# Layer 0's feed-forward network of a two-layer backbone in eighths of Strassen's products, mixed with the second matrix

## The chip, the cores and the metric

The kernel runs on one core of a Trainium2 chip. The metric is the device time of one execution in microseconds (us). A core has five engines that work through queues of their own, in order: TensorE (PE, with the weight loads PEld), VectorE (DVE), ScalarE (ACT), GpSimd (POOL) and SyncE (SP), which here issues the transfers. Line numbers such as L313 are those of the kernel file.

## The reference

Two layers over 512 latent tokens and 256 context tokens of width 1024. Each has a token mixer (windowed attention in layer 0, differential attention in layer 1) and a feed-forward network with a squared relu, hidden width 4096. All is float32.

```python
def sqrelu_mlp(h, w1, w2):
    return jnp.square(jax.nn.relu(h @ w1)) @ w2
...
        mod_x = jax.nn.silu(c) @ w_ada[i] + b_ada[i]
        sh1, sc1, g1, sh2, sc2, g2 = jnp.split(mod_x[:, None, :], N_MOD, axis=-1)
...
        x = layer_norm(alpha * x + g1 * ax, ln1_g[i], ln1_b[i])
        fx = sqrelu_mlp(x * (1.0 + sc2) + sh2, mlp_w1[i], mlp_w2[i])
        x = layer_norm(alpha * x + g2 * fx, ln2_g[i], ln2_b[i])
```

The context tokens go through layer 0 in the same way, with modulation of their own; layer 1 gives the latent tokens only. So layer 0's network works on 768 tokens, layer 1's on 512.

## The kernel before

**Products.** TensorE takes each float32 operand as a high and a low part: `wsplit` loads 128x1024 of a weight (`w_raw`), ScalarE rounds it to the high part `w_h` (L264), and VectorE subtracts to get the low part `w_l` (L313). `mm3` (L323) then makes three matmuls: high by high, high by low, low by high (L324 to L326).

**Layer 0's network, `mlp` (L681).** The 4096 hidden values are 32 blocks of 128, in four chunks of eight. For each chunk the first matrix is applied block by block (`h_ps<-hx0m`, 8 steps of the inner dimension, tokens in two cuts of 384), the result goes through relu on ScalarE, a square on VectorE (first chunk) or GpSimd (the others) and a split into `hid`. Then `tok_product` applies the second matrix for that chunk: for each half of the output columns (512) and each of the six token blocks, into `y_ps`, with four weights. The sums over chunks are kept in `fx` (VectorE adds `fx<-y_ps,fx`), the residual in `acc`.

**Layer 1's network, `mlp_pipe` (L768)**, works otherwise. Hidden blocks 0 to 5 are plain products. From there on, pairs `q` = 3 to 15 of hidden blocks take Strassen's seven block products in place of eight: the pair's 256 hidden values, the 1024 inner values and the tokens are each halved, sums of the weight's blocks are made on GpSimd (`w_sum`, `w_raw`), sums of the tokens' blocks once at the start (`token_sums`), and each half weight `w_half` of 512 columns is split on ScalarE and VectorE. The second matrix is mixed in: `pair` runs its products with "half-steps" of the second matrix between them (a half-step is one weight by one token block, six matmuls of 512 columns).

**The modulation's rows, `ada_rows` (L405).** While layer 0's network runs, VectorE computes the modulation of layer 0's last gate and of all of layer 1: 56 units of a 128x1024 piece of `w_adaT`, each multiplied by a row of silu(c) (`cB`) and reduced, once for the latent tokens or twice (context as well, then the first result goes to `ada_pr`). It is a generator; each `next` on it issues one unit: one transfer of 512 KB and one or two reductions. `mlp` calls it once for six of eight blocks in a chunk, and in the first four token blocks of each half of the second matrix.

**What sets the order.** `Flow` is a planner: jobs are generators that yield conditions, and its model of times (a clock `T`, an entry for each engine) decides which job goes on next. The order of TensorE's instructions is as the planner writes them. All engines take their queues in the order in which they were issued. Rings (`Ring`) and tile pools limit how far loads run ahead: three `w_raw` tiles, four pairs of `w_h` and `w_l`, and the modulation's units take their piece from the same three `w_raw` tiles as the weights.

Of the kernel before, what the change touches and what calls it, by code (L numbers as in the profile page):

```python
# [38 lines left out]
NRAW, NH, NQ = 3, 4, 4  # L39
# [195 lines left out]
def hybrid_block(ctx: ExitStack, tc: tile.TileContext, t: dict, out: bass.AP):  # L235
# [51 lines left out]
    rwh, rhalf = Ring(fl, NH), Ring(fl, NQ)  # L287


    xraw = {"n": 0, "pool": None}  # L290

# [113 lines left out]
    def ada_rows(pool, c_rows):  # L405
        cB = [bcast_load(pool, c_rows[s:s + 1], f"cB{s}") for s in range(2)]
        yield
        for l, m in [(0, 5)] + [(1, m) for m in (1, 0, 2, 4, 3, 5)]:
            mod = mods[l][:, m]
            n = 2 if l == 0 or m < 2 else 1  # L410
            for k in range(KT):
                raw, rg, rr = raw_tile()
                d = dma(1024, [rg], out=raw, in_=t["w_adaT"][l, m, k])
                for s in range(n):
                    to = pool.tile([P, D], F32, name="ada_pr", tag="xr", bufs=2) if s == 0 and n == 2 else raw
                    d = dv(1024, [d], nc.vector.tensor_tensor_reduce, out=to, in0=raw, in1=cB[s], scale=1.0, scalar=0.0,
                           op0=ALU.mult, op1=ALU.add, accum_out=mod[:, k, s:s + 1])
                d.ring = rr
                if k == KT - 1:
                    d = ada_bias(l, m, slice(0, KT), mod[:, :, 0:n], mod[:, :, 0:n], d)  # L420
                    if m in (2, 5):
                        fl.add(ada_gate(l, m, d), 0)
                    ada_done.add((l, m))
                yield
# [98 lines left out]
    def ln_job(pool, acc, tb, hx, A, B, ready, st, dep, keep=None):  # L523
# [4 lines left out]
        for q in range(2):  # L528
# [7 lines left out]
            if keep is not None:  # L536
                v = keep.rearrange("p (k t) -> p k t", t=P)[:, 4 * q:4 * q + 4]
            else:
                v = pool.tile([P, 4, P], F32, name="hx_v", tag="tmp", bufs=2)
# [25 lines left out]
    def gated_add(pool, give, acc, half, pt, p, gate, last, scale=1.0):  # L565
        cs_ = slice(half * 512, (half + 1) * 512)
        tm = pool.tile([P, 512], F32, name="g_tmp", tag="tmp", bufs=2)
# [26 lines left out]
    def tok_product(pool, src, W, seq, acc, gates, done=None, st=None, scale=1.0, extra=None, pre={}, sink=None,  # L594
# [5 lines left out]
        for i, (half, tb) in enumerate(seq):  # L600
# [8 lines left out]
            if fine and i == len(seq) - 1:  # L609

                for c in range(2):
# [16 lines left out]
                    tm = pool.tile([P, 256], F32, name="g_tmp", tag="tmp", bufs=2)  # L628
# [52 lines left out]
    def mlp(l, hx, ready, apool, pool, ntok, acc, gates, done, extra, res, XR=0):  # L681
        ntb = ntok // P
        first = [slice(i, i + 256) for i in range(0, ntok, 256)]

        parts = [slice(0, 512)] if ntok <= 512 else [slice(0, ntok // 2), slice(ntok // 2, ntok)]
        fx = [pool.tile([P, D], F32, name="fx", tag="fx", bufs=ntb) for _ in range(ntb)]


        def sum_up(ch, gates):
            def sink(tb, half, pt, p, give):  # L690
                x = fx[tb][:, half * 512:half * 512 + 512]
                if ch == 0:
                    give(ac(512, [p], nc.scalar.copy, out=x, in_=pt))
                    if res:
                        res.pop(0)()
                    return
                d = dv(512, [p], nc.vector.tensor_tensor, out=x, in0=pt, in1=x, op=ALU.add)
                give(d)
                if ch == 2:
                    c = slice(half * 512, half * 512 + 512)  # L700
                    g = gates[0 if tb < NXB else 1][:, c]
                    d = gp(pool2(512), [d], nc.gpsimd.tensor_tensor, out=x, in0=x, in1=g, op=ALU.mult)
                    gp(pool2(512), [d], nc.gpsimd.tensor_tensor, out=acc[tb][:, c], in0=acc[tb][:, c], in1=x, op=ALU.add)
            return sink

        row_gates = gates
        for ch in range(4):
            if l == 0 and ch == 1:
                st2["second"] = True
# [1286 lines left out]
```

## Time and profile before

| | |
|---|---|
| time, median of 3 runs | 1663.5 us (1660.76 to 1663.76) |
| the profiled execution: its time, its span | 1662.87 us, 1661.0 us |
| TensorE, VectorE, ScalarE, GpSimd busy | 1597.7, 1026.7, 726.0, 386.2 us |
| granted clock, mean over the span | 0.992 |
| layer 0's network on TensorE | about 349 to 907 us |
| layer 1's network on TensorE | about 1290 to 1661 us |

Shares of busy time are means over stages with different limits; the views by stretch of time and the waits of one engine tell which engine sets the pace in a stage. The names left of the arrow are what an instruction writes, those right of it what it reads; the engine that ended an idle time stands behind its own arrow.

### The profile page before, as it was taken

The page shows a single profiled execution, that of the slowest core. Times are in us where ns is not written, and L with a number is a line of the kernel's source. Part 1 is how long each engine was busy: PE and PEld are TensorE (multiplying, and loading weights), DVE is VectorE, ACT ScalarE, POOL GpSimd, SP SyncE. Part 2 cuts the span into 40 slices and gives each one's busy share as a digit, 9 for nine tenths or more (in the row PEclk, how much of TensorE's full clock was granted, in tenths as well). Part 3 has the DMA queues.
Part 4 walks back from the last instruction along what each step waited for, and adds up shares of the span by engine and source line. Part 5 has one row for each costly group of instructions (what it writes and reads, how often), then busy time and mean ns, then how long its engine had stood idle before and what let it go on. Part 6 is the DMA issues. An engine that isn't in the chain of part 4 may idle for free.

```text
span 1661.0 us, 24864 instructions
## 1 busy us (share of the span) xinstructions
PE 1597.7 (96%) x9621; PEld 1404.3 (85%) x9621; DVE 1026.7 (62%) x1863; ACT 726.0 (44%) x1528; POOL 386.2 (23%) x342
## 2 busy tenths in 40 slices
PE   7899999999999999999999999999989899999997
PEld 5788777789889889979978999899877789888886
DVE  4655676668855344444346777777665975666576
ACT  3465675362323113212216555556552744445550
POOL 1333454100002101243220122220100022222363
PEclk9999999999999999999999999999999999999999
DMA  9110550524444234334222122211123233333321
GB/s 373 41 51 33 179 178 26 193 81 146 134 151 158 98 127 150 104 114 139 92 77 100 60 72 69 71 48 39 48 74 130 89 127 102 102 102 102 102 77 51
DMA packets 57245, 174.84 MB, mean 105 GB/s; under 512 B 7144, under 2 KB 13096, under 8 KB 57128
## 3 DMA queue, kind: packets, MB, share of 16 engines
q1 hardware_dynamic: 57128, 173.27, 30.9%
q8 instruction: 75, 1.23, 0.3%
q14 instruction: 42, 0.34, 0.1%
HBM read 165.35 MB, written 7.90 MB: 104 GB/s over the span
## 4 chain that ended last, share of the span: by engine, by line
PE 72%; DVE 11%; ACT 5%; issue 5%; DMA 4%; POOL 3%; SPq 0%; DVEq 0%; POOLq 0%; ACTq 0%
PE y_ps L326 9%; PE y_ps L325 9%; PE y_ps L324 9%; PE h_ps L324 7%; PE h_ps L325 7%; PE h_ps L326 7%; PE qkv_ps L324 2%; PE qkv_ps L325 2%; PE qkv_ps L326 2%; PE o_ps L1369 2%; PE s_ps L1685 2%; DVE w_l L313 2%; PE pT_ps L1387 2%; DMA w_raw<-in_w 2%; PE o_ps L1723 1%
## 5 line engine op out<-in xcount | busy, mean ns | idle before, releaser
L264 ACT CAST w_h<-w_raw 128x1024 fp32r<-128x1024 f32 (+1 forms) x159 | 159.0, 1008 | 287.4 <-PE y_ps L326 136.2
L313 DVE TENSOR_TENSOR w_l<-w_raw,w_h 128x1024 fp32r<-128x1024 f32 (+1 forms) x159 | 193.1, 1224 | 146.8 <-ACT w_h L264 146.5
L325 PE MATMUL y_ps<-w_l,hid 128*128 128x512 f32 (+1 forms) x648 | 254.5, 393 | 2.9 <-DVE w_l L313 2.7
L326 PE MATMUL y_ps<-w_h,hid 128*128 128x512 f32 (+1 forms) x648 | 254.4, 393 | 0.3 <-DVE hid L260 0.2
L324 PE MATMUL y_ps<-w_h,hid 128*128 128x512 f32 (+1 forms) x648 | 254.3, 392 | 0.0
L326 PE MATMUL h_ps<-hx0m,w_l 128*128 128x384 f32 (+1 forms) x528 | 176.3, 334 | 1.3 <-DVE w_l L313 1.1
L324 PE MATMUL h_ps<-hx0m,w_h 128*128 128x384 f32 (+1 forms) x528 | 176.3, 334 | 0.0
L325 PE MATMUL h_ps<-hx0m,w_h 128*128 128x384 f32 (+1 forms) x528 | 175.9, 333 | 0.0
L325 PEld LDWEIGHTS y_ps<-w_l,hid 128*128 128x128 f32 x648 | 122.1, 188 | 30.5 <-DVE w_l L313 5.3
L326 PEld LDWEIGHTS y_ps<-w_h,hid 128*128 128x128 f32 x648 | 122.0, 188 | 28.7 <-DVE hid L260 1.2
L324 PEld LDWEIGHTS y_ps<-w_h,hid 128*128 128x128 f32 x648 | 122.2, 189 | 25.5 <-ACT w_h L264 0.2
L268 POOL TENSOR_TENSOR relu<-relu 128x768 f32<-128x768 f32 x24 | 42.7, 1779 | 367.0 <-ACT relu L264 367.0
L324 PE MATMUL qkv_ps<-w_h,hx 128*128 128x384 f32 (+1 forms) x384 | 127.5, 332 | 0.2
L325 PE MATMUL qkv_ps<-w_l,hx 128*128 128x384 f32 (+1 forms) x384 | 122.9, 320 | 0.8 <-DVE w_l L313 0.8
L326 PE MATMUL qkv_ps<-w_h,hx 128*128 128x384 f32 (+1 forms) x384 | 122.5, 319 | 0.0
L268 POOL TENSOR_TENSOR e<-e,sm 128x512 f32<-128x512 f32 (+2 forms) x96 | 92.6, 977 | 109.5 <-DVE sm L260 85.2
L326 PEld LDWEIGHTS h_ps<-hx0m,w_l 128*128 128x128 f32 x528 | 99.7, 189 | 2.5 <-DVE w_l L313 2.5
L324 PEld LDWEIGHTS h_ps<-hx0m,w_h 128*128 128x128 f32 x528 | 99.9, 189 | 0.2
L325 PEld LDWEIGHTS h_ps<-hx0m,w_h 128*128 128x128 f32 x528 | 99.8, 189 | 0.1
L260 DVE TENSOR_TENSOR fx<-y_ps,fx 128x512 f32<-128x512 f32 x68 | 46.7, 687 | 76.8 <-PE y_ps L326 76.8
L260 DVE CUSTOM_DVE_ANT_0 w_raw<-w_raw,cB 128x1024 f32<-128x1024 f32 x56 | 76.0, 1359 | 25.5 <-DMA w_raw<-in_w_adaT 25.3
L268 POOL TENSOR_TENSOR rope<-rope,rope 128x256 f32<-128x256 f32 (+1 forms) x40 | 33.8, 846 | 216.4 <-DVE rope L260 175.2
(252 smaller groups left out, 3713.8 us busy)
## 6 DMA issues: line engine op xcount, KB each, us to landing
w_raw<-in_w SPq DMA_DIRECT2D x128, 512.0 KB, 3.6
w_raw<-in_w_adaT SPq DMA_DIRECT2D x56, 512.0 KB, 3.5
w_raw<-in_w_ada SPq DMA_DIRECT2D x24, 512.0 KB, 4.1
w_raw<-in_b_w SPq DMA_DIRECT2D x32, 384.0 KB, 3.3
raw<-in_w_ada SPq DMA_DIRECT2D x16, 512.0 KB, 9.6
w_raw<-in_a_wq SPq DMA_DIRECT2D x8, 512.0 KB, 4.6
w_raw<-in_a_wo SPq DMA_DIRECT2D x8, 512.0 KB, 4.5
w_raw<-in_b_wo SPq DMA_DIRECT2D x8, 512.0 KB, 3.8
```

The costliest lines, as they stand in the source:

```text
L260: fn(**kw)
L264: fn(**kw)
L268: fn(**kw)
L313: last["split"] = nc.vector.tensor_tensor(**kw)
L324: nc.tensor.matmul(out=o, lhsT=lh, rhs=rh, start=start, stop=False, **kw)
L325: nc.tensor.matmul(out=o, lhsT=lh, rhs=rl, start=False, stop=False, **kw)
L326: last["pe"] = nc.tensor.matmul(out=o, lhsT=ll, rhs=rh, start=False, stop=stop, **kw)
L1369: nc.tensor.matmul(out=po[odd * HD:odd * HD + HD, 0:256], lhsT=vv[:, kb, kvh], rhs=pt_[:, odd * 256:odd * 256 + 256], start=(i == 0), stop ...
L1387: nc.tensor.transpose(out=pp[:, c * P:(c + 1) * P], in_=es[j][:, i * P:(i + 1) * P], identity=ident)
L1685: nc.tensor.matmul(out=sp[:, c * 512:c * 512 + 384], lhsT=qTt[:, tt, hl, qb * P:(qb + 1) * P], rhs=kS[:, tt, c * 384:c * 384 + 384], start ...
L1723: nc.tensor.matmul(out=po[:, qp * 256:(qp + 1) * 256], lhsT=vt[:, kb, vl], rhs=pt_[:, pl, a * 256:a * 256 + 256], start=(kp == 0 and pl == ...
```

## The change

`mlp` is gone, and layer 0 calls `mlp_pipe` too, with 768 tokens. What differs between the layers (buffers, how many half-steps stand in a gap, how early weights are asked for) moves to two small classes, `R0` and `R1`.

- Layer 0's first six hidden blocks are plain products, pairs 3 to 15 take seven products of 12 matmuls of 384 columns. The half-steps per pair are 4, 4 and 4 (2, 2 and 2 for the last pairs).
- The normalised tokens go to `fx` instead of a small buffer; `token_sums` makes the four sums from there. Their high and low parts need room: two take the place of `acc`, one that of a hidden tile, and one overlays a quarter of `hx0m` once the plain products have read it.
- The residual is made early and written to memory outside (`m_spill`, six tiles of 512 KB). At the last pair `tail` opens `acc` anew and reads it back; then the sums so far are multiplied by the gate and added (`fold`, 24 operations on GpSimd).
- `ada_rows` goes in two passes of 512 columns, since `cB` now has half the room. There are still 56 units of 512 KB, but each has two or four reductions of 512 columns, and the second pass adds up. `R.extra()` calls it after every half-step, and once ahead of a pair.
- The weights of the second matrix are asked for singly: one ahead (`R.ahead` is 1 in layer 0), the second just before the next pair.
- The relu's square moves from GpSimd to ScalarE, the four sums of weights per pair are on GpSimd. In layer 1 the last two products of a pair change places, and the last group of half-steps has a third early start.

```diff
     def ada_rows(pool, c_rows):
-        cB = [bcast_load(pool, c_rows[s:s + 1], f"cB{s}") for s in range(2)]
-        yield
-        for l, m in [(0, 5)] + [(1, m) for m in (1, 0, 2, 4, 3, 5)]:
...
+        todo = [(0, 5)] + [(1, m) for m in (1, 0, 2, 4, 3, 5)]
+        for h in range(2):
+            c_ = slice(h * 512, h * 512 + 512)
+            cB = [pool.tile([P, 512], F32, name=f"cB{s}", tag="tmp", bufs=tmpb[0]) for s in range(2)]
...
+                for k in range(0, KT, 2):
+                    raw, rg, rr = raw_tile()
+                    d = dma(1024, [rg], out=raw.rearrange("p (k c) -> p k c", k=2),
+                            in_=t["w_adaT"][l, m, k:k + 2, :, c_].rearrange("k p c -> p k c"))
+                    for s in range(n):
+                        for i in range(2):
+                            src = raw[:, i * 512:i * 512 + 512]
+                            to = src
+                            if s == 0 and n == 2:
+                                to = pool.tile([P, 512], F32, name="ada_pr", tag="tmp", bufs=tmpb[0])
+                            d = dv(512, [d], nc.vector.tensor_tensor_reduce, out=to, in0=src, in1=cB[s], scale=1.0,
+                                   scalar=0.0, op0=ALU.mult, op1=ALU.add, accum_out=mod[:, k + i, s:s + 1])
...
-    def mlp(l, hx, ready, apool, pool, ntok, acc, gates, done, extra, res, XR=0):
...
+        def fold(half, tb, d):
+            cs_ = slice(half * 512, half * 512 + 512)
+            x, g = fx[tb][:, cs_], gates[0 if tb < NXB else 1]
+            d = gp(pool2(512), [d], nc.gpsimd.tensor_tensor, out=x, in0=x, in1=g[:, cs_], op=ALU.mult)
+            gp(pool2(512), [d], nc.gpsimd.tensor_tensor, out=acc[tb][:, cs_], in0=acc[tb][:, cs_], in1=x, op=ALU.add)
...
+        def steps(n):
+            for _ in range(n):
+                for x in ys:
+                    if x == "half":
+                        break
+                    yield x
+                R.extra()
...
+            yield from plain((0, 1), cuts, step=R.step)
+            R.swap()
+            for ft in range(2, 6):
+                yield from plain((ft,), [t1, t2], sums, (3, 3, 2, 1)[ft - 2])
...
         y_weights(0, 0)
-        weights(3, NQ)
-        y_weights(0, 1)
-        yield from steps(ys, 8)()
+        weights(3, 4)
+        y_weights(0, 1, R.ahead)
+        yield from steps(2 * ntb)
         for q in range(3, 16):
...
             def ahead():
-                weights(q + 1, NQ)
-                if q < 15:
-                    y_weights(*((q - 1) // 2, (q - 1) % 2) if q < 14 else (6, 1))
-            yield from pair(q, steps(ys, n), ahead)
-        yield from steps(ys, 99)()
+                weights(q + 1, 4)
+                if q < 14:
+                    y_weights((q - 1) // 2, (q - 1) % 2, R.ahead)
+                elif l or q == 15:
+                    y_weights(6, 1, R.ahead)
+                if q == 15:
+                    R.tail()
+                R.extra()
+            m = R.mixes[q < 14]
+            if q < 15:
+                y_weights((q - 2) // 2, q % 2)
+            yield from pair(q, lambda i: steps(m[i]), ahead)
...
+        class R0:
+            rhalf = Ring(fl, 3)
+            mixes = ((2, 2, 2, 0), (4, 4, 4, 0))
+            p3_first, gate_at, res = True, 16, None
+            ahead, done = 1, 0
...
+            def step(self):
+                tb, self.done = self.done, self.done + 1
+                d = residual(acc[tb], gx, gc, last["pe"])
+                dma(D, [d], out=m_spill[tb], in_=acc[tb])
...
+            def tail(self):
+                p_ = open_top("mlp0c")
+                acc[:] = [p_.tile([P, D], F32, name="acc0", tag="acc", bufs=NTB) for _ in range(NTB)]
+                for tb in range(NTB):
+                    dma(D, [], out=acc[tb], in_=m_spill[tb])
+
+            def extra(self):
+                next(filler, None)
```

How the units stand among VectorE's other work before, in the first chunk of the network (`ISA` rows are reductions, `mods` rows their accumulator reads; the numbers tell tiles apart):

```order
L313 TENSOR_TENSOR w_l_4465<-w_raw_4463,w_h_4464 128x1024
L260 ISA ada_pr_4459,mods0_81<-w_raw_4457,cB0_4318 128x1024
L260 ISA mods0_81 128x1
L260 TENSOR_TENSOR relu_4452<-relu_4452 128x768
L260 ISA w_raw_4457,mods0_81<-w_raw_4457,cB1_4320 128x1024
L260 ISA mods0_81 128x1
L260 TENSOR_TENSOR hid_4057<-relu_4452,hid_4057 128x768
L260 ISA ada_pr_4495,mods0_81<-w_raw_4493,cB0_4318 128x1024
L260 ISA mods0_81 128x1
L260 ISA w_raw_4493,mods0_81<-w_raw_4493,cB1_4320 128x1024
L260 ISA mods0_81 128x1
L313 TENSOR_TENSOR w_l_4535<-w_raw_4533,w_h_4534 128x1024
```

Between two weights stand two units with four reductions. In the changed kernel, on VectorE, the end of what stands ahead of the second weight (`w_l_4826`) of the second group of the second matrix:

```order
L260 ISA ada_pr_4818,mods1_82<-w_raw_4816,cB0_4655 128x512
L260 ISA mods1_82 128x1
L260 ISA ada_pr_4820,mods1_82<-w_raw_4816,cB0_4655 128x512
L260 ISA mods1_82 128x1
L260 ISA w_raw_4816,mods1_82<-w_raw_4816,cB1_4656 128x512
L260 ISA mods1_82 128x1
L260 ISA w_raw_4816,mods1_82<-w_raw_4816,cB1_4656 128x512
L260 ISA mods1_82 128x1
L314 TENSOR_TENSOR w_l_4826<-w_raw_4824,w_h_4825 128x1024
L260 TENSOR_TENSOR w_half_4833<-w_raw_4059,w_half_4833 128x512
```

This is the last of the units; from the square of the last plain block (`relu_4600`) to `w_l_4826` there are 36 reductions. The next such weights are `w_l_5109`, `w_l_5428` and `w_l_5740`, with 28, 40 and 34 reductions ahead of each, counted from the one before; then 14, and none after pair 6.

On SP, the transfers of the same place (`in_w_adaT` are the units, `in_w2` the second matrix, `in_w1` the first) before:

```order
L275 DMA w_raw_4463<-in_w1 128x1024
L275 DMA w_raw_4493<-in_w_adaT 128x1024
L275 DMA w_raw_4527<-in_w_adaT 128x1024
L275 DMA w_raw_4533<-in_w1 128x1024
L275 DMA w_raw_4563<-in_w_adaT 128x1024
```

and in the changed kernel:

```order
L275 DMA w_raw_4786<-in_w_adaT 128x2x512
L275 DMA w_raw_4801<-in_w_adaT 128x2x512
L275 DMA w_raw_4816<-in_w_adaT 128x2x512
L275 DMA w_raw_4824<-in_w2 128x1024
L275 DMA w_raw_4877<-in_w_adaT 128x2x512
L275 DMA w_raw_4892<-in_w_adaT 128x2x512
L275 DMA w_raw_4903<-in_w_adaT 128x2x512
L275 DMA w_raw_4058<-in_w1 128x1024
```

Eleven units stand in a row ahead of `w_raw_4824` there. TensorE reads this weight in the first half-steps after two products of pair 3:

```order
L326 MATMUL y_ps_4870<-w_l_4644,hid_4054 128x512
L327 MATMUL y_ps_4870<-w_h_4643,hid_4054 128x512
L325 MATMUL y_ps_4870<-w_h_4825,hid_4055 128x512
L326 MATMUL y_ps_4870<-w_l_4826,hid_4055 128x512
L327 MATMUL y_ps_4870<-w_h_4825,hid_4055 128x512
```

The first half-step's weight (`w_h_4643`, `w_l_4644`) is followed by the second; the second matmul there needs the low part `w_l_4826`.

More of the change, by code (lines that the diff above doesn't have):

```diff
@@ L991, in last_y, with before @@
             early = []
-            y_weights(6, 1)
-            y_weights(7, 0)
-            for tb in range(2):
+            def before(tb):
                 yield sm_.ok
@@ L1000, in last_y @@
                 early.append((pt, slot))
+            y_weights(6, 1)
+            y_weights(7, 0)
+            yield from before(0)
+            yield from before(1)
+            if not gates:
+                gates.extend((yield from get_gates()))
+                for half in range(2):
+                    for tb in range(ntb):
+                        fold(half, tb, None)
             for tb in range(ntb):
@@ L1006, in last_y @@
                     p = y_half(7, 0, tb, i, pt, i == 0, i == 1, tb == ntb - 1)
[L1007 removed]
+                final(0, tb, pt, p, slot)
             y_weights(7, 1)
+            yield from before(2)
             for tb in range(ntb):
[L1010 to L1011 removed]
+                end = tb == ntb - 1 and l == 1
+                if tb < 3:
                     pt, slot = early[tb]
@@ L1037, in last_y @@
                 done(tb, st[tb], r)
-        def steps(gen, n):
-            def mix():
-                for _ in range(n):
-                    for x in gen:
-                        if x == "half":
-                            break
-                        yield x
-            return mix
-        order = [(c, half, tb) for c in range(7) for half in range(2) for tb in range(ntb)][:-ntb]
-        sums = token_sums()
-        yield from plain(range(4), [slice(i, i + 256) for i in range(0, ntok, 256)])
@@ L1069, in mlp_pipe @@
+        for x in ys:
+            if x != "half":
+                yield x
         yield from last_y()
@@ L1477, in main0 @@
                 scale_inplace(b_, ALPHA)
-            res = [lambda tb=tb: residual(acc[tb], gx, gc, last["pe"]) for tb in range(NTB)]
-            yield from mlp(0, hx, ready, apool, pool, TOK, acc, g2, done2, filler, res, D)
+            R = R0()
+            R.pool = pool
+            R.A4 = [apool.tile([P, 2, 2, TOK], F32R, name="hid", tag="A", bufs=4) for _ in range(4)]
+            R.raws = [pool.tile([P, 1024], F32, name="w_raw", tag="raw", bufs=2) for _ in range(2)]
+            yield from mlp_pipe(0, hx, ready, TOK, acc, g2, done2, fx, T0, R)
         def g2():
```

356 lines of the change are left out of this document (184 added, 172 removed).

## The prediction

> **What bounds the kernel now.** I read the page's first part and its chain of waits, then the busy time by stretch, then TensorE's waits in layer 0's feed-forward network.
>
> ```profile
> PE 1597.7 (96%) x9621; PEld 1404.3 (85%) x9621; DVE 1026.7 (62%) x1863; ACT 726.0 (44%) x1528; POOL 386.2 (23%) x342
> PE 72%; DVE 11%; ACT 5%; issue 5%; DMA 4%; POOL 3%; SPq 0%; DVEq 0%; POOLq 0%; ACTq 0%
> ...
> core 0: us, PE busy (x) PEld busy (x) DVE busy (x) ACT busy (x) POOL busy (x), PEclk, DMA share, GB/s
> 430.00:907.00 477.00, 473.61 (x2340) 420.95 (x2339) 233.30 (x309) 119.17 (x167) 88.76 (x60) 1.00 0.35 117
> ```
>
> TensorE is busy 96% of 1661.0 us. From 430 to 907 us, which is the stretch that the change rebuilds, it is busy 473.61 of 477.00 us at full clock, and VectorE is busy only 233.30, under half. So in that stretch TensorE's work is the time, and work removed from TensorE is time gained as long as nothing else becomes late. Its waits there are small:
>
> ```profile
> PE xn_t L534 <- ACT hx_v L264: 3.8, 2, 2.5
> PE y_ps L325 <- DVE w_l L313: 1.7, 2, 1.3
> PE h_ps L326 <- DVE w_l L313: 1.1, 3, 0.4
> ```
>
> The columns are us in total, how many, the longest. The second and third rows matter most: where TensorE waits in a product, it is for the low part of a weight, w_l, that VectorE subtracts. That dependency is the one to follow through the change.
>
> **What is removed.** The rows give start, duration and engine; two pairs of rows, each pair from one unbroken run, give the pace.
>
> ```profile
> 499.96 0.33 PE L324 MATMUL h_ps<-hx0m,w_h 128*128 128x384 f32 x1
> 502.04 0.33 PE L324 MATMUL h_ps<-hx0m,w_h 128*128 128x384 f32 x1
> ...
> 894.15 0.39 PE L325 MATMUL y_ps<-w_l,hid 128*128 128x512 f32 x1
> 896.47 0.39 PE L326 MATMUL y_ps<-w_h,hid 128*128 128x512 f32 x1
> ```
>
> Twelve starts apart, 2.08 us: 0.1733 us for a matmul of 384 columns. Ten apart, 2.32 us: 0.232 us for 512 columns. The change computes 13 pairs of hidden blocks with 7 block products of 12 matmuls in place of 8: 13 x 12 = 156 matmuls of 384 columns fewer, 156 x 0.1733 = **27.0 us** off TensorE. All its other counts stay. The same numbers give the new rhythm: a product is 12 x 0.1733 = 2.08 us, a half-step of the second matrix 6 x 0.232 = 1.39 us, so a pair with its 12 half-steps takes 7 x 2.08 + 12 x 1.39 = **31.3 us** of TensorE.
>
> **What VectorE gets, and when.** The modulation units are cut in halves: 80 reductions of 1024 columns become 160 of 512, each with its accumulator read. One unit is called after every half-step, so all 56 are queued between the last plain product and pair 6, where they used to be spread over the whole network. VectorE takes its queue in order, and the queue puts the second weight of every second-matrix group behind all the units called since the weight before. The prices:
>
> ```profile
> L313 DVE TENSOR_TENSOR w_l<-w_raw,w_h 128x1024 fp32r<-128x1024 f32 x64 | 81.5, 1280 | 93.3 <-ACT w_h L264 93.3
> L260 DVE TENSOR_TENSOR hid<-relu,hid 128x768 fp32r<-128x768 f32 x32 | 30.5, 954 | 36.5 <-ACT hid L264 36.5
> L260 DVE TENSOR_TENSOR fx<-y_ps,fx 128x512 f32<-128x512 f32 x24 | 16.5, 688 | 56.9 <-PE y_ps L326 56.9
> ...
> L260 DVE TENSOR_TENSOR w_half<-w_raw,w_half 128x512 fp32r<-128x512 f32 x65 | 58.0, 899 | 13.6 <-ACT w_half L264 11.1
> L260 DVE TENSOR_TENSOR w_half<-w_sum,w_half 128x512 fp32r<-128x512 f32 x26 | 20.9, 802 | 22.5 <-ACT w_half L264 22.5
> L260 DVE TENSOR_TENSOR relu<-h_ps,relu 128x256 f32<-128x256 f32 x39 | 16.4, 421 | 15.8 <-ACT relu L264 14.9 <-PE h_ps L326 0.5 <-issue 0.3
> ...
> 399.11 0.95 DVE L260 TENSOR_TENSOR relu<-relu 128x768 f32<-128x768 f32 x1
> 399.98 1.22 DVE L260 CUSTOM_DVE_ANT_0 w_raw<-w_raw,cB 128x1024 f32<-128x1024 f32 x1
> 401.13 0.95 DVE L260 TENSOR_TENSOR hid<-relu,hid 128x768 fp32r<-128x768 f32 x1
> ...
> 129.85 0.74 DVE L260 CUSTOM_DVE_ANT_0 e<-s_ps,mask,nsink 128x512 f32<-128x512 f32 x1
> 130.51 0.08 DVE L260 DVE_READ_ACCUMULATOR2_ANT nm<- 128x1 f32 x1
> 130.51 0.75 DVE L260 CUSTOM_DVE_ANT_0 e<-s_ps,mask,nsink 128x512 f32<-128x512 f32 x1
> ...
> 1443.28 0.68 DVE L260 TENSOR_TENSOR fx<-y_ps,fx 128x512 f32<-128x512 f32 x1
> 1443.88 3.32 DVE L260 TENSOR_TENSOR w_half<-w_raw,w_half 128x512 fp32r<-128x512 f32 x2
> ```
>
> No row shows a reduction of 512 columns from SBUF; the attention's custom operation of that size is nearest. Low prices are from start to start: 0.66 us for it (129.85 to 130.51, where the accumulator read adds nothing), 0.60 for a plain operation of 512, 0.87 of 768 (399.11 to 399.98), 1.15 of 1024. High prices are whole durations: 0.75 + 0.08 = 0.83, 0.69, 0.95 and 1.28. An operation of 384, between the rows of 256 (0.421) and 512, I put at 0.47 to 0.55.
>
> Now stage by stage, with counts from the order of instructions. T is the end of the last plain product. *Stage 1*: TensorE does 12 half-steps (16.7 us), two products of pair 3 (4.16) and the half-step of weight 0 (1.39); at T + 22.3 us it needs w_l_4826. The square of the last plain block can start on VectorE only after T plus ScalarE's relu:
>
> ```profile
> 550.86 0.81 ACT relu L264
> ```
>
> From that square to w_l_4826 stand 36 reductions, two operations each of 1024, 768 and 512, and one of 384: 23.8 + 2.3 + 1.7 + 1.2 + 0.5 = 29.5 us low, 36.3 high, plus 0.8: a stall of 8.0 to 14.8 us. *Stage 2*, to w_l_5109 one pair later: 28 reductions, 27.1 to 32.6 us against 31.3: stall 0 to 1.3, and VectorE at most 1.4 us ahead, since the hidden values of pair 3 stand just before it in the queue. *Stage 3*, to w_l_5428: 40 reductions, 13 operations of 512 (now with the additions to fx), three of 384, two each of 1024 and 768: 40.0 to 48.2 against 31.3, so 7.3 (with those 1.4 us) to 17.0. *Stage 4*, to w_l_5740: 34 reductions and as much besides, with ten tiny operations: 36.7 to 45.0, so 5.4 to 13.7. *Stage 5* has 14 reductions, 20.8 to 25.0 us, which fit; after it the units are used up and VectorE has slack in every pair. Sum of stalls: **20.7 to 46.8 us**. I take a third of the way up, 29.4, because the spacing rows say more about a full queue than durations do. Behind the waiting matmul stand all others, and behind them the additions to fx and relu, which wait for TensorE; so late work of VectorE isn't won back.
>
> GpSimd's four additions per pair are new too. In layer 1 they run so:
>
> ```profile
> 1443.67 1.29 POOL L268 TENSOR_TENSOR w_sum<-w_raw 128x512 f32<-128x512 f32 x1 [13.24 <-DMA w_raw<-in_w]
> 1445.04 1.62 POOL L268 TENSOR_TENSOR w_raw<-w_raw 128x512 f32<-128x512 f32 x1
> ```
>
> Beside them the two w_half of 1443.88 took 3.32 us, where 1.3 is usual: 2 us lost. The least is nothing (no overlap), the most 4 us for four additions. The group rows, nearest, give 5 x (0.899 - 0.688) + 2 x (0.802 - 0.688) = 1.3 us per pair: over the three stages that stall, 4 us. Stalls with this: **33.4 us**.
>
> **The clock.** Each of three long stalls costs a restart as well.
>
> ```profile
> 355.17 1.43 PE L534 MATMUL xn_t<-identr,acc 128*128 128x128 f32 x8 [2.48 <-ACT hx_v L264]
> 356.61 0.41 PE L325 MATMUL h_ps<-hx0m,w_h 128*128 128x256 f32 x1
> 358.75 0.41 PE L326 MATMUL h_ps<-hx0m,w_l 128*128 128x256 f32 x1
> ...
> 362.78 0.28 PE L326 MATMUL h_ps<-hx0m,w_l 128*128 128x256 f32 x1
> 363.95 0.28 PE L324 MATMUL h_ps<-hx0m,w_h 128*128 128x256 f32 x1
> ```
>
> After an idle of 2.48 us ten matmuls took 2.14 us; later, ten took 1.17. Twelve ran so slowly: 12 x 0.097 = 1.2 us, three times **3.6 us** (0 if the stalls come in small pieces).
>
> [...]
>
> **Edits that I put at little.** *Start*: the normalised rows go to fx in place of two hx_v buffers, so TensorE's waits for hx_v (3.8 us in two, one of them with its restart of 1.2) can go: 0 to -5.0; but 12 residual operations move in there too, ahead of subtractions that plain products need. I take **-2**. *Residual outside*: 6 stores and 6 loads of 512 KB; the stores have the whole network, the loads start in the last pair.
>
> ```profile
> w_raw<-in_w SPq DMA_DIRECT2D x128, 512.0 KB, 3.6
> L268 POOL TENSOR_TENSOR acc<-acc,fx 128x512 f32<-128x512 f32 x20 | 31.5, 1574 | 1.5
> L268 POOL TENSOR_TENSOR fx<-fx,g 128x512 f32<-128x512 f32 x12 | 15.5, 1293 | 35.6 <-DVE fx L260 35.6
> ```
>
> The 24 folds on GpSimd are 12 x 1.29 + 12 x 1.57 = 34 us. The first token block is through after 8 x 1.29 + 2 x 1.57 = 13.5 us from its start, after the last early half-steps; TensorE has 24 more half-steps of its own then (33 us), so the folds run under it. Without that cover the rest of them would be seen, up to some 8 us if the loads, queued on SP ahead of the weight of the last group, land late: 0 to +8, I take **0**. *Layer 1*: a product order swapped and an early group more; its waits are around 1 us each, so 0 +- 2: **0**.
>
> **Sum**: -27.0 + 33.4 + 3.6 - 2 = **+8.0 us** on the profiled execution's 1662.87 us (0.6 below the runs' median of 1663.5): **1671 us**. Lowest bounds: -27.0 + 20.7 - 5.0 = -11.3, so 1652; highest: -27.0 + 46.8 + 12 (GpSimd) + 3.6 = +35, so 1698.
>
> **Rivals.** *A, the units are hidden* (other side): the stalls vanish if a reduction of 512 columns costs under (22.3 - 0.8 - 5.7) / 36 = 0.44 us in stage 1, and (31.3 - 13.6) / 40 = 0.44 in stage 3. For it: halving the columns may save more than the nearest row shows. Against: 1024 columns take 1.15, half of that is 0.58. It gives 1662.9 - 27.0 - 2 = 1634. Chance 0.12. *B, stalls near their low bounds*, with the start won in full: 1652 to 1661; chance 0.15. *C, GpSimd holds VectorE* for the measured 2 us per two additions, 4 us in each of three stages rather than 1.3: +8, so 1679, and with high prices up to 1690. Chance 0.16.
>
> [...]
>
> *D, the tail isn't covered*: the loads of the residual delay the last weight, up to +8 on top: 1679. Against it: the 3.6 us landing row. Chance 0.07.
>
> **The numbers.** The forecast, that stalls on w_l outweigh the matmuls saved, has 0.50 and a range of its own of 1662 to 1685. About 0.2% (3.3 us) is the least that a measurement of this kernel tells from no change. Faster: A, and two thirds of B, and a little of the forecast's lower edge, 0.25. Same: 0.17, from B's top and the forecast's low end. Slower: 0.58. The range, 1648 to 1690, leaves out A and the top of C.
>
> **What would show it.** In the profile after: TensorE's waits for w_l at y_ps in layer 0 grown from 1.7 to some 30 us, in three or four pieces of 5 to 15 us, all between about 420 and 560 us; VectorE near 100% there, below 60% from 600 us on; a dip of the granted clock after each piece. Right on the saving: 156 matmuls fewer at 0.173 us. Wrong, if those waits stay under 10 us (A), if reductions of 512 columns take under 0.5 us start to start, or if the waits come at the last groups, on acc or the last weights (D).

## The result: slower by 1.8%, and the profile after

The changed kernel takes 1692.2 us (median of 4 runs, 1690.9 to 1694.6) against 1663.6 us before: a ratio of 1.0177, 95% interval 1.0159 to 1.0194. The sign was as forecast, the size wasn't: +28.6 us instead of +8, and outside the range, whose upper end was 1690. The profiled execution has a span of 1689.1 us, 28.1 more than the one before.

The page of the changed kernel, its first part and the granted clock in 40 slices of 42 us:

```profile
PE 1578.0 (93%) x9465; PEld 1388.1 (82%) x9465; DVE 1131.7 (67%) x2204; ACT 792.2 (47%) x1683; POOL 445.6 (26%) x364
PE   7899999999687899999999899999989899999997
...
PEclk9999999999798899999999999999999899999998
```

TensorE has exactly 156 matmuls fewer (9621 to 9465) and is busy 20 us less, but the span has grown. The hole is in slices 11 to 14, right behind the plain products. TensorE's waits between 340 and 960 us, changed kernel (us in total, how many, the longest; the last row is already in layer 1's attention):

```profile
PE y_ps L325 <- ACT w_h L264: 26.3, 4, 11.9
PE y_ps L326 <- DVE w_l L314: 10.1, 6, 2.7
...
PE kT_ps L1650 <- DVE nlam L1613: 3.1, 1, 3.1
```

The same stretch by time, changed kernel (busy us and count for each engine, granted clock, share of the DMA engines, GB/s):

```profile
core 0: us, PE busy (x) PEld busy (x) DVE busy (x) ACT busy (x) POOL busy (x), PEclk, DMA share, GB/s
405.00:600.00 195.00, 157.45 (x711) 135.92 (x710) 168.56 (x418) 57.14 (x95) 25.06 (x16) 0.89 0.62 202
600.00:860.00 260.00, 258.24 (x1299) 234.44 (x1298) 125.25 (x166) 103.56 (x163) 55.73 (x39) 1.00 0.23 77
```

From 405 to 600 us TensorE stands still for 195.00 - 157.45 = 37.6 us. Behind 600 us, where the units are used up, it is nearly as busy as before. The waits themselves, in TensorE's timeline of the changed kernel (start, duration, in brackets the idle time ahead and what ended it):

```profile
425.38 0.50 PE L326 MATMUL y_ps<-w_l,hid 128*128 128x512 f32 x1 [1.54 <-DVE w_l L314]
438.67 0.80 PE L325 MATMUL y_ps<-w_h,hid 128*128 128x512 f32 x1 [11.87 <-ACT w_h L264]
440.48 0.79 PE L326 MATMUL y_ps<-w_l,hid 128*128 128x512 f32 x1 [1.01 <-DVE w_l L314]
...
477.51 0.50 PE L325 MATMUL y_ps<-w_h,hid 128*128 128x512 f32 x1 [3.89 <-ACT w_h L264]
479.84 0.80 PE L326 MATMUL y_ps<-w_l,hid 128*128 128x512 f32 x1 [1.82 <-DVE w_l L314]
...
521.89 0.79 PE L325 MATMUL y_ps<-w_h,hid 128*128 128x512 f32 x1 [7.61 <-ACT w_h L264]
525.07 0.80 PE L326 MATMUL y_ps<-w_l,hid 128*128 128x512 f32 x1 [2.39 <-DVE w_l L314]
...
559.11 0.44 PE L327 MATMUL h_ps<-hx0m,w_half 128*128 128x384 f32 x1 [3.58 <-DVE w_half L260]
567.13 0.64 PE L325 MATMUL y_ps<-w_h,hid 128*128 128x512 f32 x1 [2.96 <-ACT w_h L264]
568.39 0.80 PE L326 MATMUL y_ps<-w_l,hid 128*128 128x512 f32 x1 [0.62 <-DVE w_l L314]
```

They come in the four groups that the prediction named: 14.4, 5.7, 10.0 and 7.2 us. But most of the first three was ended by w_h, not w_l, and the longest single wait of the fourth by a half weight. For the wait of 11.87 us the weight hadn't even been loaded. Its transfer on SP's queue (changed kernel, timeline of the queue):

```profile
405.87 25.28 SPq L275 DMA_DIRECT2D w_raw<-in_w_adaT  x9
433.83 0.34 SPq L275 DMA_DIRECT2D w_raw<-in_w  x1
```

TensorE needed the weight at 426.8 us (438.67 less 11.87); its load was issued at 433.83, behind units whose own loads waited for a `w_raw` tile, that is for VectorE to reduce an earlier unit. What SP's queue waited for from 405 to 600 us shows it (`mods` and `ada_half` are the results of the reductions):

```profile
SPq L275 <- DVE mods L260: 59.8, 29, 8.5
SPq L275 <- DVE ada_half L260: 56.2, 27, 5.9
```

By these rows SP stands for 116 of the 195 us before a load because no reduction has freed a tile yet.

### The profile page after: what moved, and what is told of

Read it like the earlier page. It is cut to its first block, busy times and chain, and to the rows that moved or that the text cites. A ratio compares the mean times of both kernels' runs of the same rounds, so it can differ in the third digit from the quotient of the medians.

```text
span 1689.1 us, 25129 instructions
## 1 busy us (share of the span) xinstructions
PE 1578.0 (93%) x9465; PEld 1388.1 (82%) x9465; DVE 1131.7 (67%) x2204; ACT 792.2 (47%) x1683; POOL 445.6 (26%) x364
## 5 line engine op out<-in xcount | busy, mean ns | idle before, releaser
L325 PE MATMUL y_ps<-w_h,hid 128*128 128x512 f32 (+1 forms) x648 | 256.7, 396 | 27.3 <-ACT w_h L264 26.3
L326 PE MATMUL y_ps<-w_l,hid 128*128 128x512 f32 (+1 forms) x648 | 257.0, 397 | 10.1 <-DVE w_l L314 10.1
L268 POOL TENSOR_TENSOR w_sum<-w_raw 128x512 f32<-128x512 f32 x52 | 94.8, 1822 | 501.5 <-DMA w_raw<-in_w 435.5
L314 DVE TENSOR_TENSOR w_l<-w_raw,w_h 128x1024 fp32r<-128x1024 f32 (+1 forms) x133 | 163.3, 1237 | 73.3 <-ACT w_h L264 72.7
L260 DVE TENSOR_TENSOR w_half<-w_raw,w_half 128x512 fp32r<-128x512 f32 x130 | 103.9, 803 | 86.3 <-ACT w_half L264 86.0
L326 PEld LDWEIGHTS y_ps<-w_l,hid 128*128 128x128 f32 x648 | 124.5, 192 | 34.7 <-DVE w_l L314 12.7
L264 ACT CAST w_half<-w_raw 128x512 fp32r<-128x512 f32 x130 | 79.8, 619 | 125.9 <-PE h_ps L327 75.4
L260 DVE TENSOR_TENSOR fx<-y_ps,fx 128x512 f32<-128x512 f32 x110 | 75.6, 687 | 68.9 <-PE y_ps L327 68.5
L264 ACT ACTIVATE relu<-relu 128x384 f32<-128x384 f32 (+3 forms) x104 | 69.5, 671 | 50.9 <-DVE relu L260 49.5
L260 DVE CUSTOM_DVE_ANT_0 w_raw<-w_raw,cB 128x512 f32<-128x512 f32 x112 | 77.0, 725 | 12.5 <-DMA w_raw<-in_w_adaT 12.4
L264 ACT ACTIVATE e<-e,nm 128x513 f32<-128x513 f32 (+2 forms) x96 | 65.9, 687 | 32.8 <-DVE nm L260 26.0
L264 ACT COPY relu<-h_ps 128x384 f32<-128x384 f32 (+1 forms) x78 | 32.8, 421 | 92.9 <-PE h_ps L327 92.3
L325 PE MATMUL h_ps<-hx1m,w_half 128*128 128x256 f32 x260 | 73.0, 281 | 3.0 <-ACT relu L264 2.8
```

Source lines behind the costliest of these rows:

```text
L260: fn(**kw)
L264: fn(**kw)
L268: fn(**kw)
L314: last["split"] = nc.vector.tensor_tensor(**kw)
L325: nc.tensor.matmul(out=o, lhsT=lh, rhs=rh, start=start, stop=False, **kw)
L326: nc.tensor.matmul(out=o, lhsT=lh, rhs=rl, start=False, stop=False, **kw)
```

## The experiments

**First question: does the loss come from crammed units, and through what?** Two runs spread them, one orders both weights early, one makes the reductions short.

Every third call (and, in `e_every2`, every second):

```diff
             def extra(self):
-                next(filler, None)
+                self.calls += 1
+                if self.calls % 3 == 0:
+                    next(filler, None)
```

> The modulation's units are issued at every third call instead of every call, so that they spread over all pairs (about 17 reductions per pair in place of 28 to 40). Theory V (VectorE's queue is overfull in the first pairs): per pair 17 x 0.61 = 10 us beside some 17 us of other work fits into the 31.3 us of TensorE, so the 37.6 us of waits between 405 and 600 us and the 12.7 us at half clock go: about 1642 us, faster than before. Rival S (the split weights come late because SP's queue and the three w_raw tiles are shared, whatever VectorE does): the loads of units still stand between the weights', waits fall by about a third only, 1675 us. Rival E (the loss lies elsewhere, in the residual's way outside and the end of the network): 1680 us or more.

> Units at every second call: about 26 reductions in each of the first pairs (units with two results), 16 us beside 17 us of other work against 31.3 us. Theory V: just over full, waits of a few us in the first three or four pairs, about 1646 us, 2 to 6 us above every third call. Rival S: 1680 us. Rival E: 1682 us or more.

Measured: 1664.6 us for every third call (ratio to before 1.0015, 1.0000 to 1.0030) and 1672.8 for every second (1.0073, 1.0042 to 1.0103). So the cramming costs 28 us, but neither the expected 1642 nor the 1646 of every second call is reached, and every second call is nearer to Rival S's 1680. In `e_every3` TensorE waits less, and for something else:

```profile
405.00:600.00 195.00, 185.09 (x904) 164.67 (x903) 136.10 (x275) 73.42 (x117) 29.21 (x20) 0.99 0.43 141
...
PE h_ps L325 <- DVE relu L260: 11.9, 5, 3.0
```

The products of a pair now wait for `relu`, five times up to 3 us. VectorE isn't full there (136 of 195 us): at one of these waits it stands for 4.1 us, up to 517.84, at the head of its queue before a `w_half` from `w_sum`, which waits for GpSimd's sums, which wait for the pair's load on SP. Theory V alone is too simple.

Short reductions, 32 columns instead of 512, with all transfers:

```diff
-                            src = raw[:, i * 512:i * 512 + 512]
+                            src = raw[:, i * 512:i * 512 + 32]
...
```

> All 56 units and their transfers stand where the change puts them, but each reduction covers 32 columns of the 512 (part of the modulation is left out). Theory V: a reduction takes some 0.15 us in place of 0.61, 140 of them give back 60 us to VectorE in the first four pairs, the waits go: about 1642 us. Rival S (transfers and their tiles): SP's queue is as before, so at least half of the waits stays, 1670 us or more.

Both weights of a group asked for early:

```diff
-            ahead, done = 1, 0
+            ahead, done = 2, 0
```

> Both weights of a group are asked for early, ahead of the pair before, in place of one early and one late; the units stay crammed. Theory Q (only the late weight's place in the queue matters): the waits go almost entirely, about 1650 us. Theory V in its strict form (the queue's total work matters): from the end of the plain products to the fourth group VectorE has some 136 us of work in 116 us of TensorE's, so about 20 us of waits stay, about 1670 us.

`e_short_reduce` took 1675.8 us: Rival S, which asked for 1670 or more with at least half of the waits left, and not Theory V's 1642. `e_both_ahead` took 1693.3 us (two runs), no better than the change, and both theories on it fail. Its waits only move: for `w_h` 9.7 us in one, for `relu` 11.9 in three products and 8.5 ahead of the modulation's gate, 41.6 us in the 200 us behind the plain products. A weight that is asked for early seems to take a tile and a place in the queue from another.

**Second question: transfers or reductions?** Three more runs: a quarter of each transfer, a quarter of the units, and the units placed elsewhere.

```diff
-                    d = dma(1024, [rg], out=raw.rearrange("p (k c) -> p k c", k=2),
+                    d = dma(1024, [rg], out=raw[:, 0:256].rearrange("p (k c) -> p k c", k=2),
...
-                for k in range(0, KT, 2):
+                for k in range(KT - 2, KT, 2):
...
```

(the first is `e_short_dma`, the second `e_few_units`)

> Units as in the change, reductions of 512 columns as before, but each unit's transfer carries a quarter (128 KB; the reduction reads 128 columns four times over, so the modulation is not computed). Theory V: VectorE's work is as in the change, waits fall little, 1680 to 1692 us. Rival S: a quarter of the transfer time, so the units' wait for their own loads (14 us of VectorE's idle time) goes and weights behind them come sooner, 1670 us.

> One of four units only, reductions and transfers both (14 units of 56; the modulation is mostly left out). This shows what the network itself costs without the cramming. If all that is lost in the pairs comes from the units: waits of under 5 us between 405 and 860 us, about 1645 us (1692 - 37.6 - 12.7, and 3 for the 14 units). If the new network also waits by itself (half weights through GpSimd's sums, two tiles for the pair's weights): as every third call, 1660 us or more.

And, with the whole modulation, the units right behind the weights of the next pair:

```diff
+            R.on = True
             ahead()
             yield from mix(2)
+            R.on = False
...
             def extra(self):
-                next(filler, None)
+                if self.on:
+                    next(filler, None)
```

> Units are issued only in the third gap of a pair, right behind the point where the next pair's and group's weights are asked for: five per pair, none in the first twelve half-steps. Theory M (mixed: an overfull VectorE queue early, plus weights that queue on SP and in the raw tiles behind units everywhere): fewer weights stand behind units, so it beats every third call by some 5 to 10 us, about 1655 us. Theory V alone (VectorE's total work per pair): five units per pair are as good as 4.3, 1664 us as measured for every third call, or some us more.

Times: 1681.5 us (`e_short_dma`, in Theory V's range), 1643.5 (`e_few_units`, near the expected 1645), 1647.7 (`e_units_after_w1`; ratio 0.9906, 0.9870 to 0.9942; better than Theory M's 1655). The stretch from 405 to 600 us, one row each for `e_short_reduce`, `e_short_dma`, `e_few_units` and `e_units_after_w1`:

```profile
405.00:600.00 195.00, 174.57 (x808) 152.24 (x807) 96.44 (x429) 63.48 (x106) 24.81 (x18) 0.94 0.63 208
```

```profile
405.00:600.00 195.00, 165.76 (x765) 143.50 (x764) 175.69 (x428) 62.22 (x102) 24.55 (x16) 0.90 0.32 96
```

```profile
405.00:600.00 195.00, 186.66 (x918) 166.64 (x917) 108.27 (x213) 76.40 (x122) 28.99 (x20) 0.97 0.32 103
```

```profile
405.00:600.00 195.00, 193.96 (x963) 174.17 (x962) 135.15 (x271) 76.73 (x121) 29.46 (x20) 1.00 0.44 143
```

TensorE's idle time, from its busy time: 37.6 us in the change, 20.4 with short reductions, 29.2 with short transfers, 8.3 with a quarter of both, 1.0 with the units placed behind the weights. (For a quarter of both under 5 were expected: 14 units still leave one wait of 6.3 us for a w_h.) So short reductions give back 17 us and short transfers 8; a quarter of the units gives back 29, more than the two together. With short reductions VectorE is busy only 96 of 195 us and 20 us of waits remain, so VectorE's work alone isn't the cause: it is the chain unit's load, tile, reduction, next load, which holds SP's queue and the three tiles that the weights use as well. Shortening one link hands the wait to the next, as SP's queue shows with short reductions in the same stretch (`e_short_reduce`):

```profile
SPq L275 <- DMA w_raw<-in_w_adaT: 64.8, 36, 4.6
SPq L275 <- DVE mods L260: 28.6, 30, 6.8
```

Here SP waits 64.8 us for a unit's own transfer to land, where it was 17.3 us in the change, and less for the reductions. `e_units_after_w1` does the whole modulation, moves as many bytes per us as the kernel before (143 against 136 GB/s there) and has hardly a stall. Spread nearly as thinly, the units cost 1664.6 us at every third call and 1647.7 behind the weights: these 17 us hang on which loads stand ahead of which, not on how many units there are. How the loss divides between the queue's order and the tiles was not tried.

**Third question: the attention of layer 1 and the end of layer 0's network.** From the last product of layer 0's network to the first of layer 1's, 398.7 us before are 409.1 us after. One run, on top of every third call, takes out the third early start of the last group:

```diff
-            yield from before(2)
...
-                if tb < 3:
+                if tb < 2:
...
```

> Every third call as before, and the third early start of the last group of half-steps taken out again (two, as in layer 1 before). If the third early start is behind the growth of layer 1's attention (399 us from the last product of layer 0's network to the first of layer 1's before, 409 after): back to about 400 us there, and 1655 us. If not: within 3 us of every third call's 1664 us.

1664.9 us (ratio 1.0008, 0.9989 to 1.0026): no difference from every third call. (The early start moves time within layer 1 only: behind the last product come 9.9 us without it and 11.6 with it, in layer 1's network 352.1 and 349.2.) What the trace showed next was a wait in the attention's output product, changed kernel:

```profile
1304.38 0.62 PE L325 MATMUL y_ps<-w_h,oT 128*128 128x512 f32 x1 [1.90 <-ACT w_h L264]
```

and on SP's queue the loads ahead of it:

```profile
1286.58 3.19 SPq L275 DMA_DIRECT2D w_raw<-in_w  x3
1290.11 3.51 SPq L275 DMA_DIRECT2D acc<-x_res  x4
...
1294.16 0.72 SPq L275 DMA_DIRECT2D w_raw<-in_b_wo  x1
```

In the kernel before the same queue reads:

```profile
1262.67 0.33 SPq L275 DMA_DIRECT2D w_raw<-in_b_wo  x1
...
1264.17 8.97 SPq L275 DMA_DIRECT2D w_raw<-in_w  x4
```

The last weight of the output product is loaded behind three weights of the next network, while before it stood ahead of them. In layer 1 every fourth load goes to a tile of its own, and which loads these are follows from a count that runs through the whole kernel. The change makes another number of loads from it in layer 0. So the count alone was moved, in the change and in the best variant:

```diff
         open_top(None)
         tmpb[0] = 2
+        xraw["n"] += 2
```

> The change as it is, with that count alone moved on by two. Theory R: 1692.2 less 5 to 6 us, 1686 to 1688 us. Rival: 1692 us.

> Units right behind the weights of the next pair, as measured (1647.7 us), with the count that picks the weight tile (every fourth load goes to a tile of its own in layer 1) moved on by two between the layers, so that the last weight of the attention's output is again loaded ahead of the next network's first weights. Theory R (the change moved this count, and so the order of the loads in layer 1): the wait of 2.2 us with 0.7 behind it and the 6.8 us at half clock there go: 5 to 6 us off, 1642 us, and 402 us rather than 409 between the last product of layer 0's network and the first of layer 1's. Rival (the wait comes from GpSimd or VectorE being late): no change, 1648 us.

`x_change_phase`: 1682.6 us (ratio 1.0128, 1.0109 to 1.0147), 9.6 us less than the change, where 5 to 6 were expected; the attention is back at 399.9 us, and the last weight of the output product stands ahead of the next network's again (`x_change_phase`):

```profile
1286.21 0.33 SPq L275 DMA_DIRECT2D w_raw<-in_b_wo  x1
...
1287.71 8.85 SPq L275 DMA_DIRECT2D w_raw<-in_w  x4
```

The output product itself, from its first matmul to its last, takes 68.0 us before, 73.0 in the change and 66.3 with the count moved, so 6.7 of the 9.0 us between the two profiled executions lie where the loads were moved. The rest is what other stages gained and lost, and its cause wasn't tried. Not all of the attention's growth comes from the loads either. Ahead of the output product the stretch is 324.1 us before, 329.4 in the change and 327.0 with the count moved. There the changed kernels wait 3.1 us for the first `kT_ps` (the wait that the profile puts down to `nlam`, at 945.03 in the change), where the kernel before waited 0.8, and the clock is at half behind it for 3.4 us (0.50 granted from 946.2 to 949.6 us in the change). What makes that wait wasn't tried.

`x_units_phase`: **1638.6 us** (ratio 0.9864, 0.9846 to 0.9883), with 404.1 us of attention where 402 were expected. This version beats both kernels: the change, with the units placed behind the next pair's weights, and the count moved. Spreading and placing the units together are worth 1682.6 - 1638.6 = 44 us, of which spreading alone gave 28.

The rival on the tail, with the residual's loads issued behind the last group's first weights:

```diff
             y_weights(6, 1)
             y_weights(7, 0)
+            R.tail()
             yield from before(0)
...
-                if q == 15:
-                    R.tail()
```

> As x_units_phase, with the residual's loads issued after the loads of the last group's first weights, in place of ahead of one of them. Theory D (my rival: the loads delay that weight): the wait of 2.6 us for w_l at the last group goes and nothing takes its place, since GpSimd's folds have 33 us of products to hide under: 1640 us, 2 to 3 us off. Rival: the folds start some 7 us later and the last groups wait for them: 1645 us or more.

1640.3 us (0.9873, 0.9848 to 0.9897), the same as without it, and the wait is still there (`x_tail_late`):

```profile
832.86 0.79 PE L326 MATMUL y_ps<-w_l,hid 128*128 128x512 f32 x1 [2.47 <-DVE w_l L314]
```

The residual's loads don't cause that wait, and the folds don't show when they start 2 us later (at 811.1 us against 809.0). What delays the weight is open.

**Fourth question: a gain that no term held.** Laid segment by segment, the two profiles didn't close: TensorE did the same matmuls of 512 columns faster after the change, 0.2270 us from start to start against 0.2320 (medians over some 2200), even ahead of the network, where the code is the same. One more run of the kernel before and four runs with addresses moved:

```diff
+    pad = small.tile([P, 32], F32, name="pad", tag="pad", bufs=1)
+    nc.vector.memset(pad, 0.0)
...
-                    mod = small.tile([P, KT, 2], F32, name="ada_half", tag="ada_half", bufs=2)
+                    mod = pool.tile([P, KT, 2], F32, name="ada_half", tag="ada_half", bufs=2)
```

(the first is `p_before128` on the kernel before and `p_best128` on the best variant, with 64 in place of 32 `p_before256`; the second `p_best0`, on the best variant)

> The kernel before, unchanged, for the pace of its matmuls on this chip: in the first profile 512 columns took 0.2320 us from start to start before and 0.2270 after. If that is the chip: 0.2270 here too. If it is the kernel: 0.2320.

> The kernel before with a tile of 128 bytes per partition that nothing uses, so that the tiles of hidden values and normalised tokens (the stationary operands of the second matrix) lie 128 bytes further on, as in the changed kernel. Theory P (the pace of matmuls of 512 columns hangs on these addresses): 0.2270 us from start to start in place of 0.2320, some 2200 x 0.005 = 11 us off, 1652 us. Rival (the pace comes from something else in the change): 0.2320, 1663 us.

> As p_before128 with 256 bytes. Theory P: another pace again or one of the two, the time following it by 2200 times the difference. Rival: 1663 us.

> The best variant (units behind the next pair's weights, the tile count moved on) with the small tile ada_half in another pool, so that hidden values lie where they lay before the change. Theory P: 0.2320 us, some 11 us more, 1650 us. Rival: 1639 us.

> The best variant with 128 bytes more, the same addresses as p_before256. Theory P: the pace of p_before256. Rival: 0.2270 and 1639 us.

| run | hidden values begin at byte | us per 512 columns | time, ratio to before |
|---|---|---|---|
| x_before | 49728 | 0.2320 | 1663.4 us |
| p_before128 | 49856 | 0.2270 | 1653.3 us, 0.9950 (0.9932 to 0.9968) |
| p_before256 | 49984 | 0.2320 | 1662.9 us, 1.0006 (0.9989 to 1.0022) |
| x_units_phase | 49856 | 0.2270 | 1638.6 us, 0.9864 (0.9846 to 0.9883) |
| p_best0 | 49728 | 0.2320 | 1650.6 us, 0.9934 (0.9915 to 0.9952) |
| p_best128 | 49984 | 0.2320 | 1651.2 us, 0.9940 (0.9912 to 0.9969) |

The bytes are from the built programs; the weights that stream past (`w_h` from byte 15552) stay where they are. Other tiles that lie behind the added one move with the hidden values, so that these are the cause is argued from which tiles a matmul reads. The pace in two rows of one unbroken run, `p_before128` and then `x_before`:

```profile
341.09 0.39 PE L324 MATMUL y_ps<-w_h,hx 128*128 128x512 f32 x1
342.90 0.39 PE L326 MATMUL y_ps<-w_h,hx 128*128 128x512 f32 x1
```

```profile
339.88 0.39 PE L326 MATMUL y_ps<-w_h,hx 128*128 128x512 f32 x1
342.66 0.40 PE L326 MATMUL y_ps<-w_h,hx 128*128 128x512 f32 x1
```

Eight starts in 1.81 us are 0.226; twelve in 2.78 are 0.232. Theory P holds in `p_before128`, `p_best0` and `p_best128`; `p_before256` fits it and its rival alike. By these runs a shift of 128 bytes is worth 8 to 13 us, and the changed kernel has it from `ada_half`, a small tile of 128 bytes that moved the hidden values.

## Why the prediction was right and wrong, step by step

| step | predicted | measured |
|---|---|---|
| 156 matmuls removed | -27.0 us | 156 fewer, pace of 384 columns unchanged (median 0.1750 us): -27 |
| start | -2 | -2.3 |
| waits on weights, 405 to 600 us | 33.4 (20.7 to 46.8) | 37.6 |
| half clock behind them | 3.6 | 12.7 |
| tail | 0 | 2.7 |
| attention of layer 1 | 0, layer 1 as a whole | +10.3 |
| layer 1's network | 0 | -2.4 |
| pace of 512 columns in layer 0's network | not in the sum | -5 |
| behind the last matmul | not in the sum | +1.5 |

The measured column sums up to +28.1, as the spans say, with the -5 taken as what is left of the network's segment; the experiments on the addresses bear it out, since 1150 matmuls by 0.005 us are 5.8.

The forecast missed by 20 us. Layer 1's attention is 10 of them, the clock 9, the waits 4, the tail 3; the other rows take 6 off.

**The likeliest case was right in kind**: the matmuls saved are outweighed by waits for the second matrix's weights, in four groups between 420 and 570 us, and they are gone where the units are used up. The sum of these waits was off by 4 us only, and that was luck: two of its inner steps were wrong and covered each other. A reduction was cheaper than any price I used: most follow one another after 0.61 us (404.54 to 405.15 in the changed kernel), below my 0.66 to 0.83. And VectorE was later than I let it be:

```profile
404.54 0.68 DVE L260 CUSTOM_DVE_ANT_0 w_raw<-w_raw,cB 128x512 f32<-128x512 f32 x1
405.15 0.08 DVE L260 DVE_READ_ACCUMULATOR2_ANT mods<- 128x1 f32 x1
405.15 0.68 DVE L260 CUSTOM_DVE_ANT_0 w_raw<-w_raw,cB 128x512 f32<-128x512 f32 x1
...
410.14 0.95 DVE L260 TENSOR_TENSOR relu<-relu 128x768 f32<-128x768 f32 x1
```

I let the square of the last plain block start at T + 0.8; T was 402.9 us, and the square came at 410.1, 6.4 us late, because seven reductions and the last three token sums stood between. The first group of waits, 14.4 us, hit my high bound at prices below my low one.

**The step that failed: "is VectorE's queue in time?" was taken for "is the weight in time?"** I priced only the subtraction, and let TensorE wait some 30 us for `w_l`. It waited 10.1 us for `w_l` and 26.3 for `w_h`, since the load came late: SP's queue and the three tiles formed one chain with VectorE. VectorE, which I had near 100% there, was busy for 168.56 of 195.00 us, 86%. I had shown the eleven units ahead of `w_raw_4824` in the order of SP and put no term on it. `e_short_reduce` shows what that step was worth: with VectorE at half load, 20 us of waits remained. This step failed in the mechanism; in the sum, the two that follow failed.

**The clock was mis-sized**, 12.7 us in place of 3.6. The sum of the five stretches with the clock at half, changed kernel:

```profile
427.40:444.50 17.10, 4.82 (x11) 3.45 (x12) 16.80 (x48) 2.68 (x4) 0.00 (x0) 0.50 0.67 217
...
560.50:563.90 3.40, 3.40 (x11) 2.50 (x9) 3.32 (x10) 1.74 (x3) 0.00 (x0) 0.50 0.78 269
...
sum 44.50, PE 25.58 PEld 19.07 DVE 43.15 ACT 7.97 POOL 0.00; mean PE 5.12 PEld 3.81 DVE 8.63 ACT 1.59 POOL 0.00
```

I took one restart from the kernel before, 1.2 us after an idle of 2.48, and three of them. There were five stretches at half clock (0.50 granted), with TensorE busy for 25.6 us in them; with half of that counted as lost, an estimate from the granted clock, they cost 2.5 us each. Each stretch lasted beyond the wait. TensorE's timeline behind the wait of 11.87 us, which ended at 438.67:

```profile
441.07 0.63 PE L327 MATMUL y_ps<-w_h,hid 128*128 128x512 f32 x1
444.06 0.58 PE L325 MATMUL y_ps<-w_h,hid 128*128 128x512 f32 x1
444.71 0.40 PE L327 MATMUL y_ps<-w_h,hid 128*128 128x512 f32 x1
446.11 0.40 PE L327 MATMUL y_ps<-w_h,hid 128*128 128x512 f32 x1
```

Seven starts take 2.99 us, 0.427 us each; from 444.71 on six take 1.40, 0.233 each: the full clock is back some 5.8 us after the work began again. The five stretches last 17.1, 6.8, 10.3, 3.4 and 6.9 us, that is five, two, three, one and two times 3.4 us. So there were five in place of my three, and by the same estimate each cost 1.7 to 3.1 us (2.5 in the mean) in place of the 1.2 that I took.

**Layer 1 at nothing** is the other term that failed: 0, give or take 2 us, against 10.3 in its attention. I looked at the edits in layer 1 and its "waits around 1 us each", and not at the count of tiles that a change in layer 0 moves; moving the count gave the run 9.6 us back. **The start** of -2 was right by luck: I had expected waits for the normalised rows to go, but they are 4.2 us after (1.15 and 3.02) against 3.8 before. The restart behind them, 1.2 us, went (after the wait of 3.02 us the granted clock is 1.00, where it was 0.50 for 3.4 us before); what else made the start shorter wasn't followed up.

**The tail** held to 2.7 us, and rival D fell: in the best variant, later loads of the residual change nothing. **Rival A** (stalls hidden) is what the units' place makes of the same instructions: 1.0 us of waits, though not by cheap reductions, as I had it, but by the order. **Rival C** (GpSimd holds VectorE) has a share. The two groups of reductions from 405 to 600 us, changed kernel:

```profile
L260 DVE CUSTOM_DVE_ANT_0 w_raw<-w_raw,cB 128x512 f32<-128x512 f32 x112 | 77.0, 725 | 12.5 <-DMA w_raw<-in_w_adaT 12.4
L260 DVE CUSTOM_DVE_ANT_0 ada_pr<-w_raw,cB 128x512 f32<-128x512 f32 x46 | 35.7, 777 | 1.8 <-DMA w_raw<-in_w_adaT 1.5
```

Undisturbed ones last 0.69 us, so they lost 112 x 0.035 + 46 x 0.087 = 8 us of VectorE's time in all, between the two prices I had for GpSimd. Only ten of the 160 are slow, 0.85 to 1.78 us, and each of the ten runs beside one of GpSimd's additions, for example:

```profile
450.30 1.78 DVE L260 CUSTOM_DVE_ANT_0 w_raw<-w_raw,cB 128x512 f32<-128x512 f32 x1
449.77 1.75 POOL L268 TENSOR_TENSOR w_raw<-w_raw 128x512 f32<-128x512 f32 x1
```

What these 8 us add to TensorE's waits wasn't tried. The reductions also waited 14 us for their own loads. **Outside the sum** was a gain in the matmuls' pace that I couldn't have read from any row.

## What to carry to other kernels

Work that fills an idle engine has to be placed against the loads of the engine that sets the time: ask for each weight what stands ahead of it on the transfer queue, which tile it needs and who frees that tile, not only whether the last engine ahead of it has time. Here the same instructions cost +28 us at one place and, with one accident put right, gave about -23 us at another (8 to 13 of them from the addresses). And count what a change moves without meaning to: a running tile count set the order of loads 400 us later, and a tile of 128 bytes changed the pace of the matmuls of 512 columns by 2% (0.2270 us against 0.2320).

## What the runs showed of the hardware that wasn't expected

- Matmuls of 512 float32 columns take 0.2270 us from start to start when the stationary operands' tile begins at byte 49856 of a partition, and 0.2320 at 49728 and 49984, with the streaming weights from 15552 on. 15552 and 49856 differ by a multiple of 256 bytes, 15552 and the other two by 128 more than one: the faster pace is where both operands have the same offset in 256 bytes. Other offsets weren't tried, and what causes the difference wasn't shown.
- In layer 0's network of the changed kernel the clock was granted at 0.50 in five stretches of 17.1, 6.8, 10.3, 3.4 and 6.9 us, each a multiple of 3.4 us, all at waits of 3 to 12 us. Beyond the waits they cost an estimated 1.7 to 3.1 us each, 2.5 in the mean (half of TensorE's busy time in each).
- An accumulator read between two reductions adds nothing to their spacing in the rows shown: it starts together with the next reduction at 405.15, 0.61 us after the first, for 512 columns.
- A reduction of 512 columns that runs beside an addition of GpSimd took up to 1.78 us in place of 0.69 (ten of 160), and the addition beside it up to 1.77 in place of 1.29.
